# The first product in two halves of the tokens, the logarithm behind the conv's copies, and low halves put off in the last stage

## The chip, the cores and the metric

The kernel runs on one core of a Trainium2 chip. The time is device microseconds of one execution, the median over the runs shown. The core has TensorE (PE, matmuls), VectorE (DVE), ScalarE (ACT), GpSimd (POOL) and SyncE (SP, which here issues most DMAs); PEld is the load of the stationary operand into TensorE.

## The reference

One layer of a hybrid decoder, float32, 512 tokens of width 1024; all matrices are given in full.

```python
h = rms_norm(x, norm_g[0])
proj = h @ w_in                     # lru_x, lru_g, nsa_q, nsa_kv, nsa_gate, gla_*, merge_logit
y_a = rglru_mixer(...)              # conv of width 4, gates, linear recurrence, times gelu gate
y_b = nsa_mixer(...)                # compressed, selected and window attention, 16 heads
y_c = gla_mixer(...)                # gated linear attention in chunks of 32, with log_sigmoid decay
merged = sum of sigmoid(merge gate) * (y @ w_branch)
x = x + rms_norm(merged @ w_out, norm_g[1])
h = rms_norm(x, norm_g[2])
gt, up = split(h @ w_ffn_in)        # each 512 x 2816
x = x + rms_norm((silu(gt) * up) @ w_ffn_out, norm_g[3])
```

## The kernel before

Every operand of a product is split into two parts, a rounded high half (`hi`, `hh`, `whi`, made by a cast on ScalarE) and the remainder (`lo`, `hl`, `wlo`, made by a subtraction on VectorE or GpSimd), and each product is three matmuls that accumulate in one PSUM tile: high x high, high x low, low x high (`mm3`, whose three matmuls are L122, L123 and L124). Weights come as tiles of 128 x 1024 by DMA (`wraw`), from a pool of few buffers; each is cast (`whi`) and its remainder made (`wlo`) before TensorE can use it.

**The start** (L252 to L319, and L704 to L707). SP loads the four token tiles `xt` of 128 x 1024, then the two halves `ck_raw` of the first weight. For each token tile ScalarE sums the squares (`square`) and takes the root, VectorE makes the factor and scales the tile (`root`), and TensorE turns it in eight transposes into eight PSUM tiles `tps`, one for each 128 features, of 512 tokens each. Six matmuls on zeros (L304) stand behind the first tile's transposes. When all four tiles are turned, `hh` (ScalarE) and `hl` (VectorE) are evicted in eight instructions of 512 columns each, and then 48 matmuls of 512 columns make the first product, the keys of the compressed branch. The order in this block is the one written (`manual_schedule`); elsewhere a scheduler orders the instructions of each engine by priority and readiness.

**The recurrence's stage** goes over four pairs of channel tiles (`cp` 0 to 3). Streams of matmuls (`stream_t`) have other engines' work hung between their steps. For a pair, `conv` copies the projected input out of PSUM (L995, ScalarE), adds three shifted products (L1000, VectorE), casts (`xh`, L1002) and subtracts (`xl`, L1004), and TensorE makes the gates from both (`rips`). `z_exp` and `z_log` (L1068, L1072) are the two parts of the decay's log-sigmoid for the linear attention, four tiles of 512 columns each; both are hung on the last matmul stream of the round `cp` = 2. A change of the function of ScalarE between groups needs a table load.

**The last stage.** The products of the FFN's input are combined from seven smaller ones per tile pair (`winograd`, `product` at L1707 and L1710, 256 columns each; `after` gathers the results, where `fy` is the sum at L1719). When these run out, the product with `w_ffn_out` begins, in the same scheme: `tile_a` loads two blocks of the weight, `tile_b` a sum made earlier (`rows_d`) and makes a difference of `tile_a`'s two blocks (L1806), `pair` loads two blocks, and `split_u` casts the tile (L1779) and makes its low half (L1782). `weights()` hands out a tile and prepares up to three ahead; `use` runs the matmuls of a half tile into accumulators `acc`. In the program's order the low half of a tile stands directly behind its cast, except in one short stretch that a list `late` holds back. `fetch2` loads operands `r2` through SP, `second` splits them, `gb3` is the last norm's gain. At the end `store` writes eight blocks of 128 x 512, by ScalarE's queue for the first half of the columns and SP's for the second.

Of the kernel before, what the change touches and what calls it, by code (L numbers as in the profile page):

```python
# [14 lines left out]
OP = mybir.AluOpType  # L15
# [47 lines left out]
def hybrid_block_kernel(ctx, tc, x, rel_table, norm_g, w_in, conv_w, conv_b, lru_w_gates, lru_b_gates,  # L63
# [186 lines left out]
    with tc.tile_pool(name="pre", bufs=1) as pp:  # L250
        xts = [pp.tile([128, D], F32, name=f"xt{tb}") for tb in range(TB)]
        for tb in range(TB):  # L252
            sy.dma_start(xts[tb], x[0, tb * 128:(tb + 1) * 128, :])
        g8 = pp.tile([8, 128], F32, name="g8")
# [6 lines left out]
        for i in range(WARM):  # L261
# [4 lines left out]
        tps = [p.tile([128, S], F32, name="tps", tag=t) for p, t in  # L266
               ((pg, "g"), (po, "o"), (pt, "pt"), (pt, "pt"), (pa, "a"), (pa, "a"), (pa, "a"), (pa, "a"))]
        ck_raw = [load_raw([(lambda t: t.rearrange("p (k c) -> p k c", k=4),
                             dap(w_in, kh * 512 * INW + K_CMP, [[INW, 128], [128 * INW, 4], [1, 256]]))])
                  for kh in range(2)]  # L270
        ck = []

        def ck_split(kh):
            ck.append([t.rearrange("p (k c) -> p k c", k=4) for t in split_w(ck_raw[kh], v_)])

        with tc.manual_schedule(engines={mybir.EngineType.PE, mybir.EngineType.DVE, mybir.EngineType.Activation}):
            sss, ms, rs_ = [], [], []
# [9 lines left out]
            def root(tb):  # L287

                xt, m = xts[tb], ms[tb]
                r = pp.tile([128, 1], F32, name=f"r{tb}")  # L290
                t = pp.tile([128, 1], F32, name=f"t{tb}")
                a_.activation(r, m, AF.Sqrt)
                v_.reciprocal(r, r)
                v_.scalar_tensor_tensor(t, r, r[:, 0:1], m, op0=OP.mult, op1=OP.mult)
                v_.tensor_scalar(t, t, -0.5, 1.5, op0=OP.mult, op1=OP.add)
                v_.tensor_scalar(xt, xt, r[:, 0:1], t[:, 0:1], op0=OP.mult, op1=OP.mult)
                for ft in range(8):
                    pe.transpose(tps[ft][:, tb * 128:(tb + 1) * 128], xt[:, ft * 128:(ft + 1) * 128], ident)

            square(0)  # L300
            root(0)

            for i in range(WARM2):
                pe.matmul(tps[7][:, 384:512], wz, wz, start=True, stop=True)  # L304
            square(1)
            for tb in range(2, TB):
                square(tb)
                root(tb - 1)
# [3 lines left out]
            root(TB - 1)  # L312
            ck_split(0)
            for ft in range(8):
                a_.activation(hh[:, ft], tps[ft], AF.Copy, scale=g0[:, ft:ft + 1])
                v_.scalar_tensor_tensor(hl[:, ft], tps[ft], g0[:, ft:ft + 1], f(hh[:, ft]), op0=OP.mult,  # L316
                                        op1=OP.subtract)
                if ft == 3:
                    ck_split(1)  # L319
# [384 lines left out]

    ps0 = psum_t()
    for kh, n, k in [(0, n, k) for k in range(4) for n in range(2)] + [(1, n, k) for n in range(2) for k in range(4)]:
        (h, l), kk, c = ck[kh], kh * 4 + k, slice(n * 128, n * 128 + 128)  # L707
        mm3(ps0[n], h[:, k, c], l[:, k, c], hh[:, kk], hl[:, kk], kk == 0, kk == 7)
# [279 lines left out]
    def conv(cp, pss):  # L988
# [4 lines left out]
        for j, ps in enumerate(pss):  # L993
            ct = 2 * cp + j
            a_.activation(xc[:, j], ps, AF.Identity, scale=par[:, 24 + ct:25 + ct], bias=par[:, 32 + ct:33 + ct])  # L995
        for j, ps in enumerate(pss):
# [85 lines left out]
    for cp in range(4):  # L1082
# [4 lines left out]
        conv(cp, px)  # L1087
# [8 lines left out]
        if cp == 0:  # L1096
            lru_params()
        pm = stream_t(Y[:2], chain(lambda: lru_tanh(cp), *([z_products] if cp == 2 else [])),
                      chain(lambda: lru_exp(cp), *([z_exp, z_log] if cp == 2 else [])))
# [510 lines left out]
    fq = []  # L1610

    def f_cast(i):
        if i < len(floads):
# [7 lines left out]
    def f_lo(i):  # L1621
        if i < len(floads):
# [144 lines left out]
    late = []  # L1767

# [7 lines left out]
    def split_u(raw, n=1024):  # L1776
# [7 lines left out]
        if late:  # L1784
            late.append(low)
        else:
            low()
        return hi, lw

# [268 lines left out]
```

## Time and profile before

| | |
|---|---|
| median of 3 runs | 1201.88 us (1201.55 to 1203.12) |
| profiled execution | 1202.26 us, span 1200.6 us |
| mean granted clock of TensorE | 0.996 of full speed |
| busy: PE, PEld | 1180.5 us (98%), 1009.9 us (84%) |
| busy: DVE, ACT, POOL | 726.3 us (60%), 607.0 us (51%), 256.6 us (21%) |
| DMA | 219.30 MB, mean 183 GB/s |

The profile is of one execution; its times count from the span's start, and 1.7 us lie outside the span. A wait in it is the idle time of an engine before an instruction, put down to what came last. The end of a matmul is modelled: one of 512 columns shows 0.39 us busy, and the next starts before that is over, so the pace is read from starts. A matmul that begins after a wait shows a longer time, as it refills the pipeline. [...] The share of busy time covers stages that differ: at the start, in the conv and at the end TensorE waits, elsewhere hardly.

### The profile page before, as it was taken

The numbers are of one execution on the slowest core, as the hardware profiler recorded it, in microseconds if no ns is written. First come the engines' busy times: TensorE is split into PE (matmuls) and PEld (weight loads), VectorE is DVE, ScalarE is ACT, GpSimd is POOL, SyncE is SP. The second block draws the span as 40 slices with busy tenths as digits, with TensorE's granted clock in tenths as the row PEclk, the third lists the DMA queues.
The fourth block names the chain that finished last, engine by engine and source line by source line (L and its number), as shares of the span: only waits on it lengthen the run. The fifth ranks groups of instructions, "written<-read, shape, count | busy, mean of one in ns | idle before, by whom it ended". The sixth has DMA issues, their size and how long they took to land. (4 is left out here: it accounts for less than half of the span.)

```text
span 1200.6 us, 19226 instructions
## 1 busy us (share of the span) xinstructions
PE 1180.5 (98%) x7114; PEld 1009.9 (84%) x7114; DVE 726.3 (60%) x1417; ACT 607.0 (51%) x1165; POOL 256.6 (21%) x327
## 2 busy tenths in 40 slices
PE   9999999999999999999999999999999999989996
PEld 7898888888888878888888888887989999987785
DVE  6615556555467769465544353446786777765777
ACT  5326656565387677453434233234455565644553
POOL 1224555566213213222122222200000000000000
PEclk9999999999999999999999999999999999999999
DMA  8872765551469947885487989944246667667753
GB/s 259 236 217 83 195 222 196 179 163 40 115 153 228 246 151 215 202 201 150 132 203 179 212 196 236 214 149 134 85 123 189 207 202 212 197 193 239 244 184 123
DMA packets 203743, 219.30 MB, mean 183 GB/s; under 512 B 29170, under 2 KB 169694, under 8 KB 201424
## 3 DMA queue, kind: packets, MB, share of 16 engines
q1 hardware_dynamic: 189120, 170.87, 46.7%
q0 software_dynamic: 13936, 46.14, 18.3%
q8 instruction: 56, 0.92, 0.3%
q10 hardware_dynamic: 592, 1.05, 0.2%
q14 instruction: 39, 0.32, 0.1%
HBM read 209.83 MB, written 77.41 MB: 239 GB/s over the span
## 5 line engine op out<-in xcount | busy, mean ns | idle before, releaser
L92 DVE TENSOR_TENSOR wlo<-wraw,whi 128x1024 fp32r<-128x1024 f32 x91 | 111.8, 1233 | 113.6 <-ACT whi L91 86.9
L91 ACT CAST whi<-wraw 128x1024 fp32r<-128x1024 f32 x113 | 117.9, 1048 | 118.7 <-PE gps L897 29.6
L870 POOL COPY tick<-whi 128x1 f32<-128x1 f32 x76 | 53.8, 708 | 340.4 <-ACT whi L91 340.4
L894 PE MATMUL gps<-hh,whi 128*128 128x512 f32 x320 | 126.0, 394 | 0.0
L897 PE MATMUL gps<-hl,whi 128*128 128x512 f32 x320 | 124.5, 389 | 0.0
L1625 DVE TENSOR_TENSOR wlo<-wraw,whi 128x1024 fp32r<-128x1024 f32 x67 | 81.9, 1222 | 14.5 <-ACT whi L1616 14.0
L676 DVE COPY psb<-ptp 128x512 f32<-128x512 f32 (+2 forms) x72 | 45.4, 631 | 64.2 <-PE ptp L672 60.5
L637 ACT ACTIVATE p<-p,mx 128x384 f32<-128x384 f32 (+3 forms) x128 | 68.7, 539 | 26.7 <-DVE mx L635 26.5
L894 PE MATMUL gps<-hh,wlo 128*128 128x512 f32 x320 | 79.1, 389 | 0.0
L1616 ACT CAST whi<-wraw 128x1024 fp32r<-128x1024 f32 x67 | 70.3, 1049 | 13.4 <-DMA wraw<-t_d 12.0
L651 POOL TENSOR_TENSOR p<-p,sc 128x256 f32<-128x256 f32 (+3 forms) x64 | 76.5, 1217 | 1.9
L894 PE MATMUL gps<-yh,whi 128*128 128x512 f32 x192 | 74.9, 390 | 0.0
L897 PE MATMUL gps<-yl,whi 128*128 128x512 f32 x192 | 74.7, 389 | 0.0
L122 PE MATMUL gps<-hh,whi 128*128 128x512 f32 (+1 forms) x176 | 73.4, 418 | 0.8 <-DVE hl L316 0.8
L894 PEld LDWEIGHTS gps<-hh,wlo 128*128 128x128 f32 x320 | 60.1, 188 | 12.5
L894 PEld LDWEIGHTS gps<-hh,whi 128*128 128x128 f32 x320 | 60.1, 188 | 12.4
L897 PEld LDWEIGHTS gps<-hl,whi 128*128 128x128 f32 x320 | 60.1, 188 | 12.3
L122 PE MATMUL gps<-whi,hh 128*128 128x512 f32 (+1 forms) x192 | 69.9, 364 | 0.0
L124 PE MATMUL gps<-whi,hl 128*128 128x512 f32 (+1 forms) x192 | 68.1, 354 | 0.0
L123 PE MATMUL gps<-wlo,hh 128*128 128x512 f32 (+1 forms) x192 | 68.0, 354 | 0.0
L124 PE MATMUL gps<-hh,wlo 128*128 128x512 f32 (+1 forms) x176 | 65.7, 374 | 0.0
L123 PE MATMUL gps<-hl,whi 128*128 128x512 f32 (+1 forms) x176 | 65.5, 372 | 0.0
(442 smaller groups left out, 3061.8 us busy)
## 6 DMA issues: line engine op xcount, KB each, us to landing
wraw<-in_w_in_dram SPq DMA_DIRECT2D x44, 512.0 KB, 6.4
t_d<-in_w_ffn_in_dram SPq DMA_DIRECT2D x32, 704.0 KB, 8.0
wraw<-t_d SPq DMA_DIRECT2D x72, 256.0 KB, 3.2
wraw<-in_w_ffn_in_dram SPq DMA_DIRECT2D x70, 256.0 KB, 3.8
wraw<-in_w_in_dram SPq DMA_DIRECT2D x64, 256.0 KB, 4.5
t_d<-in_w_ffn_in_dram POOLq DMA_DIRECT2D x16, 704.0 KB, 9.2
rows_d<-in_w_ffn_out_dram POOLq DMA_DIRECT2D x22, 512.0 KB, 5.2
t_d<-t_d POOLq DMA_DIRECT2D x16, 704.0 KB, 8.2
```

The source lines that it names most:

```text
L91: a_.copy(hi, raw)
L92: lo_eng.tensor_tensor(lo, raw, f(hi), op=OP.subtract)
L122: pe.matmul(ps, lh, rh, start=first, stop=False)
L123: pe.matmul(ps, lh, rl, start=False, stop=False)
L124: pe.matmul(ps, ll, rh, start=False, stop=last)
L637: a_.activation(o, o, AF.Exp, scale=-1.0, bias=mx[:, br, gi:gi + 1], accum_out=sm[:, br, gi:gi + 1])
L651: g_.tensor_tensor(o, o, sc[:, br][:, :, None].to_broadcast([128, 2, n]), op=OP.mult)
L870: g_.tensor_copy(tick, f(hi[:, 0, 0:1]))
L894: pe.matmul(ps[n], part_[:, k, c], ah[:, kk], start=kk == 0 and part_ is h, stop=kk == 7 and part_ is l)
L897: pe.matmul(ps[n], h[:, k, c], al[:, kk], start=False, stop=False)
L1616: a_.copy(hi, raw)
L1625: v_.tensor_tensor(lo, raw, f(hi), op=OP.subtract)
```

## The change

It has four parts. At the start the loads go in the order first two token tiles, first weight half, other two token tiles, second weight half. The first product is made in two halves of the tokens (`first(i, kh)`: token half i, weight half kh), 96 matmuls of 256 columns; the first half stands between the transposes of the first two and the last two token tiles, `high` and `low` evict 256 columns at a time, two features' tiles share one PSUM tile, and the last token tile is scaled on ScalarE instead of VectorE. In the recurrence `z_log` moves from the end of round 2 into the conv of round 3, between its copies from PSUM and its shifted products. In the last stage each low half is collected in `late` and made by `lows()`, which runs at the end of each `use` and in `f_lo`; `tile_a` now also loads `tile_b`'s sum and makes the difference; `weights()` and the square root's table load are called later, `fetch2` elsewhere with four buffers for three. The stores go by SP but for one.

```diff
+        ck_raw = []
         for tb in range(TB):
             sy.dma_start(xts[tb], x[0, tb * 128:(tb + 1) * 128, :])
+            if tb % 2:
+                ck_raw.append(load_raw([(lambda t: t.rearrange("p (k c) -> p k c", k=4),
+                                         dap(w_in, tb // 2 * 512 * INW + K_CMP,
+                                             [[INW, 128], [128 * INW, 4], [1, 256]]))]))
         g8 = pp.tile([8, 128], F32, name="g8")
         a_.dma_start(g8, dap(norm_g, 0, [[128, 8], [1, 128]]))
...
-        tps = [p.tile([128, S], F32, name="tps", tag=t) for p, t in
-               ((pg, "g"), (po, "o"), (pt, "pt"), (pt, "pt"), (pa, "a"), (pa, "a"), (pa, "a"), (pa, "a"))]
+        tps = [[p.tile([128, 2, 256], F32, name="tps", tag=t) for p, t in banks] for banks in
+               (((pa, "a"), (pa, "a"), (pa, "a"), (pa, "a")), ((pt, "pt"), (pt, "pt"), (pa, "a"), (pa, "a")))]
...
             def root(tb):
-
-                xt, m = xts[tb], ms[tb]
                 r = pp.tile([128, 1], F32, name=f"r{tb}")
+                a_.activation(r, ms[tb], AF.Sqrt)
+                rs_.append(r)
+
+            def scale(tb):
+
+                xt, m, r = xts[tb], ms[tb], rs_[tb]
                 t = pp.tile([128, 1], F32, name=f"t{tb}")
-                a_.activation(r, m, AF.Sqrt)
                 v_.reciprocal(r, r)
                 v_.scalar_tensor_tensor(t, r, r[:, 0:1], m, op0=OP.mult, op1=OP.mult)
                 v_.tensor_scalar(t, t, -0.5, 1.5, op0=OP.mult, op1=OP.add)
-                v_.tensor_scalar(xt, xt, r[:, 0:1], t[:, 0:1], op0=OP.mult, op1=OP.mult)
+                if tb < TB - 1:
+                    v_.tensor_scalar(xt, xt, r[:, 0:1], t[:, 0:1], op0=OP.mult, op1=OP.mult)
+                else:
+                    v_.tensor_tensor(r, r, t, op=OP.mult)
+                    a_.activation(xt, xt, AF.Copy, scale=r[:, 0:1])
+
+            def turned(tb):
                 for ft in range(8):
-                    pe.transpose(tps[ft][:, tb * 128:(tb + 1) * 128], xt[:, ft * 128:(ft + 1) * 128], ident)
+                    pe.transpose(tps[tb // 2][ft // 2][:, ft % 2, tb % 2 * 128:tb % 2 * 128 + 128],
+                                 xts[tb][:, ft * 128:(ft + 1) * 128], ident)
+
+            def high(i, *fts):
+                for ft in fts:
+                    a_.activation(hh[:, ft, i * 256:i * 256 + 256], tps[i][ft // 2][:, ft % 2], AF.Copy,
+                                  scale=g0[:, ft:ft + 1])
+
+            def low(i, *fts):
+                for ft in fts:
+                    t = slice(i * 256, i * 256 + 256)
+                    v_.scalar_tensor_tensor(hl[:, ft, t], tps[i][ft // 2][:, ft % 2], g0[:, ft:ft + 1],
+                                            f(hh[:, ft, t]), op0=OP.mult, op1=OP.subtract)
+
+            def first(i, kh):
+                (h, l), t = ck[kh], slice(i * 256, i * 256 + 256)
+                for k, n in [(k, n) for k in range(4) for n in range(2)]:
+                    c, kk = slice(n * 128, n * 128 + 128), kh * 4 + k
+                    mm3(ps0[n][:, t], h[:, k, c], l[:, k, c], hh[:, kk, t], hl[:, kk, t], i + kk == 0, i == 1 and kk == 7)
 
             square(0)
             root(0)
+            scale(0)
+            turned(0)
 
             for i in range(WARM2):
-                pe.matmul(tps[7][:, 384:512], wz, wz, start=True, stop=True)
+                pe.matmul(tps[1][1][:, 1, 128:256], wz, wz, start=True, stop=True)
             square(1)
-            for tb in range(2, TB):
-                square(tb)
-                root(tb - 1)
+            root(1)
+            scale(1)
+            turned(1)
+            ck_cast(0)
+            square(2)
+            ck_low(0)
+            high(0, 0, 1)
+            low(0, 0, 1)
+            root(2)
+            high(0, 2, 3)
+            low(0, 2, 3)
+            first(0, 0)
+            square(3)
+            scale(2)
+            turned(2)
+            ck_cast(1)
+            high(0, 4, 5)
+            ck_low(1)
+            root(3)
+            low(0, 4, 5)
+            high(0, 6, 7)
+            low(0, 6, 7)
+            first(0, 1)
 
             for j8 in range(2):
                 g_.tensor_copy(M[:, 4 * j8, 0:1], xts[TB - 1][:, 0:1])
-            root(TB - 1)
-            ck_split(0)
+            scale(3)
+            turned(3)
             for ft in range(8):
-                a_.activation(hh[:, ft], tps[ft], AF.Copy, scale=g0[:, ft:ft + 1])
-                v_.scalar_tensor_tensor(hl[:, ft], tps[ft], g0[:, ft:ft + 1], f(hh[:, ft]), op0=OP.mult,
-                                        op1=OP.subtract)
-                if ft == 3:
-                    ck_split(1)
+                high(1, ft)
...
-
-    ps0 = psum_t()
-    for kh, n, k in [(0, n, k) for k in range(4) for n in range(2)] + [(1, n, k) for n in range(2) for k in range(4)]:
-        (h, l), kk, c = ck[kh], kh * 4 + k, slice(n * 128, n * 128 + 128)
-        mm3(ps0[n], h[:, k, c], l[:, k, c], hh[:, kk], hl[:, kk], kk == 0, kk == 7)
...
-    def conv(cp, pss):
+    def conv(cp, pss, then=None):
...
             a_.activation(xc[:, j], ps, AF.Identity, scale=par[:, 24 + ct:25 + ct], bias=par[:, 32 + ct:33 + ct])
+        if then:
+            then()
         for j, ps in enumerate(pss):
...
-        conv(cp, px)
+        conv(cp, px, z_log if cp == 3 else None)
...
         pm = stream_t(Y[:2], chain(lambda: lru_tanh(cp), *([z_products] if cp == 2 else [])),
-                      chain(lambda: lru_exp(cp), *([z_exp, z_log] if cp == 2 else [])))
+                      chain(lambda: lru_exp(cp), *([z_exp] if cp == 2 else [])))
...
     fq = []
+    late = []
+
+    def lows():
+        while late:
+            late.pop(0)()
 
     def f_cast(i):
+        if i >= len(floads) + 2:
+            return
         if i < len(floads):
...
             ahead(i - len(floads) + 1)
 
     def f_lo(i):
+        lows()
...
         def low():
             v_.tensor_tensor(lw[:, :n], raw[:, :n], f(hi[:, :n]), op=OP.subtract)
 
-        if late:
-            late.append(low)
-        else:
-            low()
+        late.append(low)
         return hi, lw
...
     def tile_a(k):
 
-        t = last["a"] = raw_tile()
+        t, tb_ = raw_tile(), raw_tile()
         sy.dma_start(t[:, 0:512], wsrc(k, 0))
         sy.dma_start(t[:, 512:1024], wsrc(NK + k, 1))
+        sy.dma_start(tb_[:, 0:512], rows_d[k * 128:k * 128 + 128, 512:1024])
+        v_.tensor_tensor(tb_[:, 512:1024], t[:, 0:512], t[:, 512:1024], op=OP.subtract)
+        last["b"] = tb_
         return split_u(t)
 
     def tile_b(k):
 
-        t, ab = raw_tile(), last["a"]
-        sy.dma_start(t[:, 0:512], rows_d[k * 128:k * 128 + 128, 512:1024])
-        v_.tensor_tensor(t[:, 512:1024], ab[:, 0:512], ab[:, 512:1024], op=OP.subtract)
-        return split_u(t)
+        return split_u(last["b"])
 
     def pair(src):
...
             mm3(bk[tt], ls[:, 0, sl, c], ls[:, 1, sl, c], wh, wl, k == 0, k == NK - 1)
+        lows()
...
     p2, p5 = [[p.tile([128, 512], F32, name="acc", tag=n) for _ in range(2)] for p, n in ((pa, "a"), (pt, "pt"))]
-    w = weights()
-    use(p5, LS1[0], 2, w, 1, 0)
+    lows()
+    use(p5, LS1[0], 2, done[0], 1, 0)
     y_half(2 * NK - 1, 0, "C", "u2")
     winograd(len(seq) - 2)
     after(*seq[-2])
-    use(p2, LS1[0], 1, w, 0, 0)
+    use(p2, LS1[0], 1, done[0], 0, 0)
     winograd(len(seq) - 1)
     after(*seq[-1])
-    a_.activation(cst[:, 2:3], cst[:, 0:1], AF.Sqrt)
+    weights()
...
     def fetch2(k):
         if k < NK - 1:
-            raw2[k] = fr.tile([128, 3, 256], F32, name="r2", bufs=3)
+            raw2[k] = fr.tile([128, 3, 256], F32, name="r2", bufs=4)
             sy.dma_start(raw2[k], raw2_d[:, k])
...
         v_.scalar_tensor_tensor(o, gained[tb, hf], rss[tb][1][:, 0:1], xres[tb, hf], op0=OP.mult, op1=OP.add)
-        (sy if hf else a_).dma_start(out[0, tb * 128:(tb + 1) * 128, c], o)
+        (a_ if (tb, hf) == (1, 1) else sy).dma_start(out[0, tb * 128:(tb + 1) * 128, c], o)
...
-    fetch2(0)
-    fetch2(1)
     for k in range(NK):
...
         if k == 4:
             second(NK - 1)
-        fetch2(k + 2)
+        if k == 0:
+            fetch2(0)
+        fetch2(k + 1)
+        if k == NK - 1:
+            a_.activation(cst[:, 2:3], cst[:, 0:1], AF.Sqrt)
...
             use(p7, LS2[k], 1, w, k % 2, k)
         if p == 1:
 
-            late.append(None)
...
             mean(2 + p)
         if p == 2:
-            for low in late[1:]:
-                low()
             store(2, 0)
             store(2, 1)
```

TensorE at the start of the program: `wz` are the zeros, `xt_112` to `xt_115` the four token tiles, `gps` the first product. The order before:

```order
L263 MATMUL gp_125<-ident,g_120 128x8
L298 MATMUL tps<-ident,xt_112 128x128 x8
L304 MATMUL tps<-wz 128x128 x6
L298 MATMUL tps<-ident,xt_113 128x128 x8
L298 MATMUL tps<-ident,xt_114 128x128 x8
L298 MATMUL tps<-ident,xt_115 128x128 x8
L122 MATMUL gps<-hh,whi 128x512
L123 MATMUL gps<-hl,whi 128x512
```

The order now (`hh,whi 128x512` at L164 belongs to the product after the first):

```order
L319 MATMUL tps<-ident,xt_112 128x128 x8
L345 MATMUL tps<-wz 128x128 x6
L319 MATMUL tps<-ident,xt_113 128x128 x8
L122 MATMUL gps<-hh,whi 128x256
L123 MATMUL gps<-hl,whi 128x256
L124 MATMUL gps<-hh,wlo 128x256
...
L319 MATMUL tps<-ident,xt_114 128x128 x8
L122 MATMUL gps<-hh,whi 128x256
...
L319 MATMUL tps<-ident,xt_115 128x128 x8
L122 MATMUL gps<-hh,whi 128x256
L164 MATMUL gps<-hh,whi 128x512 x2
L123 MATMUL gps<-hl,whi 128x256
```

The first product's matmuls, 256 columns wide, now stand in front of the transposes of the third and the fourth token tile, and behind the last transposes matmuls of the next product (L164) come between those of the first.

ScalarE in the recurrence's round 3: `yf` at the line with a table load directly ahead are the logarithms, `xc` the conv's copies, `xh` its cast. The order before:

```order
L1068 ACTIVATE yf<-yf 128x512 x4
L1072 ACT_TABLE_LOAD
L1072 ACTIVATE yf<-yf,cst 128x512 x4
L91 CAST whi<-wraw 128x1024
L1047 ACT_TABLE_LOAD
L1047 ACTIVATE a_4787<-a_4787 128x1024
L91 CAST whi<-wraw 128x1024
L984 CAST gwh<-gwr 128x512
L995 ACTIVATE xc<-gps,par 128x512 x2
L1002 CAST xh<-xc 128x512 x2
```

The order now:

```order
L1125 ACTIVATE yf<-yf 128x512 x4
L91 CAST whi<-wraw 128x1024
L1104 ACT_TABLE_LOAD
L1104 ACTIVATE a_4852<-a_4852 128x1024
L91 CAST whi<-wraw 128x1024
L1039 CAST gwh<-gwr 128x512
L1050 ACTIVATE xc<-gps,par 128x512 x2
L1129 ACT_TABLE_LOAD
L1129 ACTIVATE yf<-yf,cst 128x512 x4
L1059 CAST xh<-xc 128x512 x2
```

The table load and the four logarithms stood ahead of the root for the recurrence (`a`); they now stand behind the copies `xc` and ahead of the cast `xh`.

VectorE where the FFN's last input products end: `fy` are the sums that free TensorE's accumulators, `wlo<-wraw` low halves (at L1625, in the new kernel L1690, of FFN input weights, at L1782 or L1845 of W_ffn_out), `wraw<-wraw` the difference of two blocks. The order before:

```order
L1487 TENSOR_TENSOR am<-am 128x512
L1782 TENSOR_TENSOR wlo<-wraw,whi 128x1024
L1751 SCALAR_TENSOR_TENSOR am<-fy,fsg 128x512
L1806 TENSOR_TENSOR wraw<-wraw 128x512
L1782 TENSOR_TENSOR wlo<-wraw,whi 128x1024 x2
L1719 TENSOR_TENSOR fy<-wc,u_10699 128x256
L1719 TENSOR_TENSOR fy<-wa,p_10586 128x256
L1806 TENSOR_TENSOR wraw<-wraw 128x512
L1782 TENSOR_TENSOR wlo<-wraw,whi 128x1024
```

The order now:

```order
L1551 TENSOR_TENSOR lsf<-am,lsf 128x1024
L1690 TENSOR_TENSOR wlo<-wraw,whi 128x1024
L1544 TENSOR_TENSOR am<-am 128x512
L1862 TENSOR_TENSOR wraw<-wraw 128x512
L1845 TENSOR_TENSOR wlo<-wraw,whi 128x1024
L1816 SCALAR_TENSOR_TENSOR am<-fy,fsg 128x512
L1784 TENSOR_TENSOR fy<-wc,u_10767 128x256
L1784 TENSOR_TENSOR fy<-wa,p_10651 128x256
L1845 TENSOR_TENSOR wlo<-wraw,whi 128x1024
L1862 TENSOR_TENSOR wraw<-wraw 128x512
```

Two low halves stood in front of the last two `fy`; now none of W_ffn_out stands between `am` and these two, and the difference comes a place ahead of the low half in front of them.

## Rows read from the trace of the kernel before

**Rows 1.** The page's busy table: engine, busy us (share of the span), instructions.

```profile
PE 1180.5 (98%) x7114; PEld 1009.9 (84%) x7114; DVE 726.3 (60%) x1417; ACT 607.0 (51%) x1165; POOL 256.6 (21%) x327
```

**Rows 2.** TensorE's waits: us in total, times, longest us.

```profile
PE wa L1707 <- DVE fy L1719: 3.1, 1, 3.1
PE acc L123 <- DVE wlo L1782: 1.3, 3, 0.8
PE rips L123 <- DVE xl L1004: 1.3, 1, 1.3
...
PE tps L298 <- DVE xt L296: 0.7, 2, 0.3
```

**Rows 3.** Timeline of TensorE, start: start us, us busy, instruction, [idle, releaser].

```profile
13.37 1.09 PE L298 MATMUL tps<-ident,xt 128*128 128x128 f32 x8 [0.33 <-DVE xt L296]
15.27 0.50 PE L122 MATMUL gps<-hh,whi 128*128 128x512 f32 x1 [0.80 <-DVE hl L316]
```

**Rows 4.** Stretches: length, busy (instructions) by engine, granted clock, DMA share, GB/s.

```profile
15.20:26.20 11.00, 10.93 (x48) 9.08 (x49) 7.26 (x20) 6.01 (x10) 0.53 (x3) 1.00 0.64 154
...
1079.16:1082.57 3.41, 3.24 (x14) 3.15 (x15) 0.71 (x2) 0.28 (x1) 0.00 (x0) 0.50 0.23 80
1082.57:1126.00 43.43, 41.51 (x172) 31.25 (x171) 27.61 (x30) 21.44 (x25) 0.00 (x0) 1.00 0.74 246
```

**Rows 5.** Groups by line and shape, 13 to 24 us: busy us, mean ns, idle.

```profile
L316 DVE SCALAR_TENSOR_TENSOR hl<-tps,g,hh 128x512 fp32r<-128x512 f32 x8 | 5.4, 744 | 0.0
...
L315 ACT ACTIVATE hh<-tps,g 128x512 fp32r<-128x512 f32 x8 | 4.9, 704 | 2.0 <-PE tps L298 2.0
```

**Rows 6.** Groups by line and shape, 26.5 to 31.5 us.

```profile
L421 DVE COPY x<-gps 64x256 f32<-64x256 f32 x2 | 0.8, 421 | 1.7 <-PE gps L124 1.3 <-ACT x L421 0.4
L421 ACT COPY x<-gps 64x256 f32<-64x256 f32 x2 | 0.7, 366 | 1.2 <-DVE x L421 1.2
```

**Rows 7.** Timeline of ScalarE, the recurrence's round 3.

```profile
430.50 1.28 ACT L1072 ACT_TABLE_LOAD   x1
431.79 2.56 ACT L1072 ACTIVATE yf<-yf,cst 128x512 f32<-128x512 f32 x4
...
446.49 0.62 ACT L1002 CAST xh<-xc 128x512 fp32r<-128x512 f32 x1 [6.01 <-DVE xc L1000]
```

**Rows 8.** Timeline of VectorE, the same round.

```profile
435.33 1.23 DVE L92 TENSOR_TENSOR wlo<-wraw,whi 128x1024 fp32r<-128x1024 f32 x1 [4.48 <-ACT whi L91]
```

**Rows 9.** Timeline of TensorE, the end of the FFN's input products.

```profile
1073.25 0.28 PE L1707 MATMUL wa<-hh,whi 128*128 128x256 f32 x1
...
1074.68 0.40 PE L122 MATMUL acc<-whi,ls 128*128 128x512 f32 x1
...
1075.84 0.39 PE L124 MATMUL acc<-whi,ls 128*128 128x512 f32 x1
1079.33 0.58 PE L1707 MATMUL wa<-hh,whi 128*128 128x256 f32 x1 [3.10 <-DVE fy L1719]
...
1082.05 0.63 PE L122 MATMUL acc<-whi,ls 128*128 128x512 f32 x1
...
1096.66 0.51 PE L122 MATMUL acc<-whi,ls 128*128 128x512 f32 x1 [0.55 <-ACT whi L1779]
1097.92 0.51 PE L123 MATMUL acc<-wlo,ls 128*128 128x512 f32 x1 [0.76 <-DVE wlo L1782]
```

**Rows 10.** Timeline of VectorE there.

```profile
1077.38 1.23 DVE L1782 TENSOR_TENSOR wlo<-wraw,whi 128x1024 fp32r<-128x1024 f32 x1 [1.90 <-ACT whi L1779]
1078.53 0.42 DVE L1719 TENSOR_TENSOR fy<-wc,u 128x256 f32<-128x256 f32 x1
...
1079.19 0.68 DVE L1806 TENSOR_TENSOR wraw<-wraw 128x512 f32<-128x512 f32 x1
```

**Rows 11.** Timeline of ScalarE there.

```profile
1095.56 1.05 ACT L1779 CAST whi<-wraw 128x1024 fp32r<-128x1024 f32 x1 [3.60 <-DMA wraw<-in_w_ffn_out_dram]
```

**Rows 12.** Timeline of SP's queue there.

```profile
1088.86 0.54 SPq L1799 DMA_DIRECT2D wraw<-in_w_ffn_out_dram  x1
```

More of the change, by code (lines that the diff above doesn't have):

```diff
@@ L264, in hybrid_block_kernel, with ck_cast, ck_low @@
         v_.tensor_copy(g0, gp8[:, 0:8])
-        tps = [p.tile([128, S], F32, name="tps", tag=t) for p, t in
-               ((pg, "g"), (po, "o"), (pt, "pt"), (pt, "pt"), (pa, "a"), (pa, "a"), (pa, "a"), (pa, "a"))]
-        ck_raw = [load_raw([(lambda t: t.rearrange("p (k c) -> p k c", k=4),
-                             dap(w_in, kh * 512 * INW + K_CMP, [[INW, 128], [128 * INW, 4], [1, 256]]))])
-                  for kh in range(2)]
-        ck = []
-        def ck_split(kh):
-            ck.append([t.rearrange("p (k c) -> p k c", k=4) for t in split_w(ck_raw[kh], v_)])
+        tps = [[p.tile([128, 2, 256], F32, name="tps", tag=t) for p, t in banks] for banks in
+               (((pa, "a"), (pa, "a"), (pa, "a"), (pa, "a")), ((pt, "pt"), (pt, "pt"), (pa, "a"), (pa, "a")))]
+        ck = []
+        def ck_cast(kh):
+            hi = wpool.tile([128, 1024], F32R, name="whi")
+            lo = wpool.tile([128, 1024], F32R, name="wlo")
+            a_.copy(hi, ck_raw[kh])
+            ck.append((hi, lo))
+        def ck_low(kh):
+            hi, lo = ck[kh]
+            v_.tensor_tensor(lo, ck_raw[kh], f(hi), op=OP.subtract)
+            ck[kh] = [t.rearrange("p (k c) -> p k c", k=4) for t in ck[kh]]
         with tc.manual_schedule(engines={mybir.EngineType.PE, mybir.EngineType.DVE, mybir.EngineType.Activation}):
-            sss, ms, rs_ = [], [], []
+            ps0 = psum_t()
+            ms, rs_ = [], []
             def square(tb):
@@ L310, in hybrid_block_kernel @@
+            ck_low(1)
[4 more added lines that the diff above has]
+            first(0, 1)
             for j8 in range(2):
                 g_.tensor_copy(M[:, 4 * j8, 0:1], xts[TB - 1][:, 0:1])
-            root(TB - 1)
-            ck_split(0)
+            scale(3)
+            turned(3)
             for ft in range(8):
-                a_.activation(hh[:, ft], tps[ft], AF.Copy, scale=g0[:, ft:ft + 1])
-                v_.scalar_tensor_tensor(hl[:, ft], tps[ft], g0[:, ft:ft + 1], f(hh[:, ft]), op0=OP.mult,
-                                        op1=OP.subtract)
-                if ft == 3:
-                    ck_split(1)
+                high(1, ft)
+                low(1, ft)
@@ L321, in small_consts @@
+            first(1, 0)
+            first(1, 1)
     def small_consts(pp):
@@ L1766, in hybrid_block_kernel @@
     raws = [0]
-    late = []
     def raw_tile():
```

## Prediction

> **What bounds the kernel now.** I read the busy table first: TensorE is busy for 1180.5 us, 98% of the span [rows 1]. A change can therefore win in two ways only, by taking a wait from TensorE or by letting it run at its higher clock where it does not, and it can lose by adding matmul time. So the next view is the list of TensorE's waits [rows 2]: the longest is one of 3.1 us for a VectorE result `fy` near the end of the program, then three for a low half `wlo` (1.3 together), one for the conv's low half `xl` (1.3), and two for the normalised input `xt` (0.7). The waits on semaphores before the first product add 0.80 [rows 3]. Each of these lies in a place that the change touches, so the sum is made place by place from the timelines there. [...]
>
> **The start: the first product in halves.** Before, TensorE turns the four token tiles, waits 0.33, 0.33 and 0.80 on the way (the two of 0.33 are the 0.7 of [rows 2], the last is in [rows 3]), and from 15.27 us runs 48 matmuls in 10.93 us, 0.228 each [rows 4]. The waits sum to 1.46. After it, 96 matmuls of 256 columns. The nearest row for one is the winograd group near the end: 12 matmuls from 1073.25 to 1074.68, 0.119 each [rows 9]. So 96 x 0.119 = 11.4 us, 0.5 more than before.
> What can be won is the 1.46 us. I walked the new order by durations. The transposes of tile 1 take about as long as now (8 in 1.09 [rows 3]); then the first matmul needs one eviction `hh` of 256 columns, the second an `hl`. No row shows these; the nearest are a copy of 256 columns at 0.366 on ScalarE and 0.421 on VectorE [rows 6], and the same evictions at 512 columns, 0.704 and 0.744 [rows 5]. I take 0.48 for either, nearer to the copy plus what scaling adds. The first matmul so waits some 0.5 for `hh`, the next 0.5 for `hl`; the transposes of tile 2 wait some 0.2 for `xt`, the second four feature tiles 0.5 for `hl` behind the second `wlo` on VectorE, and those of tile 3 some 0.3 for the scaling that now runs on ScalarE. That is 2.0 us in place of 1.46: the waits are cut into more and smaller pieces, not removed. In the second half eight pairs `hh`, `hl` feed the matmuls, 0.48 + 0.48 for 0.71 us of matmuls (6 x 0.119) when they follow each other on one PSUM tile; the order puts matmuls of the next product between them, which covers it. The small loads that come later on SP can hold the conv of the compressed keys by some tenths. Sum: 0.5 + 0.5, less a little for cover: **+0.9 us**. Bounds: all waits gone, 0.5 - 1.46 = -1.0; and without the cover 8 x 0.25 = 2.0 on top, +2.9.
> A row speaks for a price of halving: 256 columns cost VectorE 0.421 and 512 cost 0.744, so two halves are 0.1 dearer than a whole [rows 5, 6]. [...]
>
> **The logarithm `z_log` moved behind the conv's copies.** Before, ScalarE runs a table load (1.28) and four logarithms (2.56) at 430.50 [rows 7], and everything behind them waits: VectorE idles 4.48 us before the `wlo` at 435.33 [rows 8], then the scan of the recurrence, the gate product and the conv follow on it, and the cast `xh` comes only after ScalarE idled 6.01 us [rows 7]. TensorE waits 1.30 for `xl` at the end of this chain [rows 2]. Taken out there, the chain comes 3.8 us earlier (1.28 + 2.56); the same 3.8 us now lie on ScalarE inside its idle 6.01, before `xh`. The next limit is the end of the stream of matmuls that TensorE is busy with until then, so only the wait goes: **-1.3 us**, bounds 0 (`xh` is late behind the logarithms) and -1.3.
>
> **The end: low halves put off.** Before, two low halves stand on VectorE ahead of the two `fy` sums. The second starts at 1077.38 after an idle 1.90 us for its cast on ScalarE; `fy` follows at 1078.53 [rows 10], and TensorE, whose last matmul before was at 1075.84, starts again at 1079.33 [rows 9]. The wait depends on the queue's order, not on VectorE's load. After it, `fy` stands ahead of that low half, and its own inputs have been ready since TensorE's last product. So the wait of 3.1 goes. Late next is the low half of the first tile of W_ffn_out: ahead of it VectorE has a `wlo` (1.23) and a difference (0.68), both in [rows 10], and then it takes 1.23 itself. I estimate 0.8 us of wait there, where 0.2 is today: +0.6.
> Without the long idle I expect the clock to stay at 1.00. Price by rows: the 12 matmuls of 256 columns from 1079.33 to 1082.05 took 2.72 us where the 12 before took 1.43 [rows 9], 1.3; with the first wide ones behind it 1.5. So -1.5. The trace's rows are that the clock fell during the wait of 3.1 and did not through the one of 0.80 at the start. [...]
> From 1082.57 to 1126.00, 172 matmuls take 43.43 us [rows 4]; at 0.228 they would take 39.2. Of the 4.2 over, 0.55 + 0.76 at 1096.66 and 1097.92 [rows 9], with 0.1 of refilling for each, belong to a tile whose load landed late: ScalarE waited 3.60 for it [rows 11], and it was issued at 1088.86 [rows 12] behind the norm's gain and three loads of `r`. The order keeps these four ahead of it, so 1.5 stays. The other 2.6 are small waits on `wlo` and casts; since the difference is now made a tile earlier and the low half is queued later, I count two thirds as gone: -1.7, bounds 0 and -2.6. Moving the square root's table load out of this stretch takes 1.28 from ScalarE in front of a cast; that is inside the same sum.
> End together: -3.1 + 0.6 - 1.5 - 1.7 = **-5.7 us**; bounds -1.5 (the long wait halves, the clock still falls) and -7.0.
>
> **The tail.** Stores go almost all by SP; issuing a transfer takes SP about half a microsecond [rows 12], no more than VectorE needs for a block of the result. ScalarE is freed of issues that nothing waits for. **0**, bounds 0.3 either way.
>
> **Sum.** The profiled execution took 1202.26 us, 1.7 more than its span and 0.4 more than the median of the runs. 1202.26 + 0.9 - 1.3 - 5.7 = 1196.2; less 0.4, **1195.8 us**.
>
> **The rivals.** *First, the forecast*: about 1195.8, own range 1193 to 1198.5. *Second, the loads rule the end*: `fy` comes early, but TensorE then waits as long for a tile of W_ffn_out, because these tiles are read on SP behind the same big transfers; the clock falls again. For it: the load in [rows 11]. Against it: that load is needed some 17 us after the long wait. Then 1202.26 + 0.9 - 1.3 - 0.4 = 1201.5. *Third, the start is dear and the small waits stay*: +2.9 at the start and -4.0 at the end: 1202.26 + 2.9 - 1.3 - 4.0 - 0.4 = 1199.5. For it: the fixed price of halves [rows 5, 6]; against it: the cover in the order. *Fourth, the clock falls in the start*: the first 48 small matmuls run between waits, at 0.227 (2.72 / 12) for 0.119, 5.2 us more: 1201.0. Against it: 0.80 us of idle did not do it before, and no wait I expect is longer. *Fifth, slower: the low halves come late*. The stage has eleven pairs of tiles of W_ffn_out and of rows made from it; a low half that now stands behind the next tile's difference (0.68) would come that much later, with 0.1 of refilling, at each pair: 11 x 0.79 = 8.7, so 1195.8 + 8.7 = 1204.5. It decides from the point at which TensorE reaches the second matmul of a tile before the low half is done. Against it: VectorE idles for the cast before such a half [rows 10], so it has room.
>
> **Chances.** Forecast 0.70, third 0.12, second 0.08, fourth 0.05, fifth 0.05. What a measurement can tell from no change is 0.2%, 2.4 us, so faster means under 1199.5. The third case lies on that line and is halved; I shift a little from the forecast, as its end term rests on an estimate of a wait that no row shows: faster 0.78, same 0.16, slower 0.06. Range 1191.5 to 1201: its lower end is the forecast with the better bounds of end and start together in part, its upper end reaches the second and fourth cases.
>
> **What would show it.** At the start: the first matmul of 256 columns near 12 us instead of 15.27, waits on `hl` and `hh` between, and the end of the first product no earlier than now. At the conv: no wait of TensorE for `xl`, and the logarithms inside ScalarE's gap before `xh`. At the end: no wait for `fy`, the granted clock 1.00 throughout, a wait under 1 us for the first `wlo` of the stage, and the late load still there some 20 us on. It is wrong if TensorE's waits in the first 35 us fall below 1 us, or if a wait of over 2 us stands anywhere behind the last product of the FFN's input.

## The result, and the profile after

Six runs of each kernel: 1195.53 us (1195.26 to 1197.66) against 1202.02 (1201.09 to 1203.12), ratio 0.9948 with a 95% interval of 0.9936 to 0.9961. The forecast was 1195.8 us. The profiled execution took 1195.47 us, span 1193.8.

The sum came out, its terms less well. Reading when the same matmul starts in both traces, counted back from the last one, gives the account by place:

| place | forecast | measured in the traces |
|---|---|---|
| start, up to the compressed keys' products | +0.9 | +2.0 |
| conv of round 3 | -1.3 | -1.6 |
| last stage | -5.7 | -7.0 |
| behind the last matmul | 0 | -0.2 |

The expectations below were written with +2.2 for the start; the two traces give +1.98. The start also moves from run to run: in the fourteen traces of this document, one and the same matmul behind it lies up to 0.7 us apart among those with the old start and up to 0.6 among those with the new one as the change has it. So its cost is known to a few tenths only.

TensorE's waits of the changed kernel, in the columns of [rows 2]:

```profile
PE acc L123 <- DVE wlo L1845: 1.7, 3, 0.8
PE tps L319 <- ACT xt L315: 1.5, 1, 1.5
PE gp L267 <- DVE wz L262: 1.2, 1, 1.2
PE gps L123 <- DVE hl L330: 0.8, 2, 0.5
PE acc L122 <- ACT whi L1842: 0.4, 1, 0.4
```

The waits for `fy` and for `xl` are gone. New is one of 1.5 us for the last token tile, in the start. The timeline of TensorE there, against [rows 3]:

```profile
11.27 0.38 PE L122 MATMUL gps<-hh,whi 128*128 128x256 f32 x1
12.16 0.39 PE L123 MATMUL gps<-hl,whi 128*128 128x256 f32 x1 [0.50 <-DVE hl L330]
...
16.57 0.39 PE L123 MATMUL gps<-hl,whi 128*128 128x256 f32 x1 [0.32 <-DVE hl L330]
...
21.07 1.09 PE L319 MATMUL tps<-ident,xt 128*128 128x128 f32 x8 [1.48 <-ACT xt L315]
```

The first product starts at 11.27 instead of 15.27, but waits of 0.50, 0.32 and 1.48 follow, 2.3 in place of 1.46. That is 0.8 of the 2.0; 0.5 are the 96 matmuls, and the other 0.7 are refilling, which is the name here for the longer time of a matmul behind a wait (0.39 us at 12.16 and 16.57 where those that follow show 0.28), and small gaps, which I did not take apart. VectorE shows where the long one is from; then GpSimd in the same stretch:

```profile
17.61 0.16 DVE L308 RECIPROCAL r<-r 128x1 f32<-128x1 f32 x1
17.80 1.57 DVE L309 SCALAR_TENSOR_TENSOR t<-r,m 128x1 f32<-128x1 f32 x1
19.40 0.15 DVE L310 TENSOR_SCALAR t<-t 128x1 f32<-128x1 f32 x1
```

```profile
16.95 2.40 POOL L92 TENSOR_TENSOR wlo<-wraw,whi 128x1024 fp32r<-128x1024 f32 x1 [6.64 <-ACT whi L91]
```

An instruction of one column took 1.57 us where its sister for the tile before took 0.22. It ended at 19.37, GpSimd's subtraction at 19.35. In the kernel before, that subtraction ran from 25.86 us on, behind all of this chain.

In the conv ScalarE does the logarithms where it idled before [rows 7]:

```profile
439.68 1.28 ACT L1129 ACT_TABLE_LOAD   x1
440.97 2.56 ACT L1129 ACTIVATE yf<-yf,cst 128x512 f32<-128x512 f32 x4
444.83 0.62 ACT L1059 CAST xh<-xc 128x512 fp32r<-128x512 f32 x1 [1.29 <-DVE xc L1057]
```

Its idle time before `xh` is 1.29 instead of 6.01, and `xh` stands 1.66 earlier although the whole stage began 2.0 later. At the end, TensorE's timeline against [rows 9], then VectorE's against [rows 10], then the stretches against [rows 4]:

```profile
1071.89 0.39 PE L122 MATMUL acc<-whi,ls 128*128 128x512 f32 x1
1072.97 0.50 PE L123 MATMUL acc<-wlo,ls 128*128 128x512 f32 x1 [0.70 <-DVE wlo L1845]
...
1076.83 0.39 PE L124 MATMUL acc<-whi,ls 128*128 128x512 f32 x1
1077.05 0.28 PE L1772 MATMUL wa<-hh,whi 128*128 128x256 f32 x1
...
1092.71 0.50 PE L122 MATMUL acc<-whi,ls 128*128 128x512 f32 x1 [0.42 <-ACT whi L1842]
1093.97 0.50 PE L123 MATMUL acc<-wlo,ls 128*128 128x512 f32 x1 [0.76 <-DVE wlo L1845]
```

```profile
1071.10 0.68 DVE L1862 TENSOR_TENSOR wraw<-wraw 128x512 f32<-128x512 f32 x1
1071.70 1.22 DVE L1845 TENSOR_TENSOR wlo<-wraw,whi 128x1024 fp32r<-128x1024 f32 x1
...
1075.87 0.42 DVE L1784 TENSOR_TENSOR fy<-wa,p 128x256 f32<-128x256 f32 x1 [2.01 <-PE wa L1772]
```

```profile
1074.00:1091.80 17.80, 17.80 (x91) 15.15 (x90) 9.28 (x12) 5.52 (x7) 0.00 (x0) 1.00 0.74 242
1091.80:1095.30 3.50, 2.32 (x10) 1.34 (x9) 3.14 (x4) 3.39 (x4) 0.00 (x0) 1.00 0.74 276
1095.30:1120.00 24.70, 24.70 (x109) 20.22 (x108) 20.59 (x23) 13.62 (x17) 0.00 (x0) 1.00 0.92 302
```

VectorE now waits for TensorE before `fy` (2.01) and not the reverse; the products run on at 1077.05; the clock stays at 1.00; the wait at the first `wlo` is there (0.70, and 0.50 us for that matmul where others show 0.39), and so is the late tile at 1092 us. Between 1095.3 and 1120 TensorE is busy throughout: all the small waits went, of which I had counted two thirds.

### The profile page after: what moved, and what is told of

It reads as the page before. It is cut to its first block, busy times and chain, and to the rows that moved or that the text cites. A ratio compares the mean times of both kernels' runs of the same rounds, so it can differ in the third digit from the quotient of the medians.

```text
span 1193.8 us, 19335 instructions
## 1 busy us (share of the span) xinstructions
PE 1177.6 (99%) x7162; PEld 1012.1 (85%) x7162; DVE 728.4 (61%) x1425; ACT 610.0 (51%) x1174; POOL 256.2 (21%) x327
## 4 chain that ended last, share of the span: by engine, by line
PE 94%; DVE 3%; ACT 1%; issue 1%; DMA 1%; SPq 0%; DVEq 0%; ACTq 0%
PE gps L949 19%; PE gps L952 10%; PE gps L122 8%; PE gps L123 7%; PE gps L124 7%; PE wa L1772 6%; PE ops L754 4%; PE s L686 3%; PE wa L1775 3%; PE ptp L732 3%; PE wc L1772 3%; PE acc L123 2%; PE acc L124 2%; PE acc L122 2%; PE gps L164 2%; PE wb L1772 1%
## 5 line engine op out<-in xcount | busy, mean ns | idle before, releaser
L92 DVE TENSOR_TENSOR wlo<-wraw,whi 128x1024 fp32r<-128x1024 f32 x89 | 109.4, 1233 | 113.7 <-ACT whi L91 84.3
L1690 DVE TENSOR_TENSOR wlo<-wraw,whi 128x1024 fp32r<-128x1024 f32 x67 | 81.9, 1223 | 14.0 <-ACT whi L1680 13.4
L122 PE MATMUL gps<-hh,whi 128*128 128x512 f32 (+1 forms) x192 | 76.6, 399 | 0.0
L123 PE MATMUL gps<-hl,whi 128*128 128x512 f32 (+1 forms) x192 | 68.7, 358 | 0.8 <-DVE hl L330 0.8
L124 PE MATMUL gps<-hh,wlo 128*128 128x512 f32 (+1 forms) x192 | 68.6, 357 | 0.0
```

The costliest lines, as they stand in the source:

```text
L92: lo_eng.tensor_tensor(lo, raw, f(hi), op=OP.subtract)
L122: pe.matmul(ps, lh, rh, start=first, stop=False)
L123: pe.matmul(ps, lh, rl, start=False, stop=False)
L124: pe.matmul(ps, ll, rh, start=False, stop=last)
L1690: v_.tensor_tensor(lo, raw, f(hi), op=OP.subtract)
```

## The experiments

Each ran in five rounds beside the kernel before; times are medians, ratios are to the kernel before. What had to be told apart: what the start costs and why, and which of the last stage's edits moved `fy`.

**The old start in the changed kernel.** All edits of the start are undone.

> The changed kernel with the start of the kernel before (four token tiles first, then 48 matmuls of 512 columns); the rest as changed. Theory: the new start costs 2.2 us, since from the end of the first product on every matmul of the changed kernel stands 2.19 us later than before, and nothing behind it depends on how the start is made. Then 1195.5 - 2.2 = 1193.3 us, and the parts in conv and last stage keep their -1.6 and -7.0. Rival: the later stages gain because the loads of the start come in another order; then the old start gives back some of it and the time lies at 1195 or above.

1196.52 us (1194.51 to 1197.68), ratio 0.9949 (0.9936 to 0.9962): by the time alone the expectation failed. The trace shows why. The stretches at the late tile:

```profile
1080.00:1092.39 12.39, 10.74 (x47) 8.35 (x46) 6.92 (x9) 4.73 (x6) 0.00 (x0) 0.99 0.90 318
1092.39:1095.81 3.42, 3.42 (x10) 2.66 (x9) 3.42 (x5) 1.05 (x1) 0.00 (x0) 0.53 0.69 208
```

```profile
1090.66 0.49 PE L122 MATMUL acc<-whi,ls 128*128 128x512 f32 x1 [0.88 <-ACT whi L1787]
1091.92 0.56 PE L123 MATMUL acc<-wlo,ls 128*128 128x512 f32 x1 [0.77 <-DVE wlo L1790]
```

Here the wait for the late tile is longer (0.88 and 0.77 where the changed kernel shows 0.42 and 0.76), and the clock falls behind it, to 0.53 over 3.42 us. The first tile's `acc` stands 2.5 us earlier than in the changed kernel, near the 2.2 expected; the late tile takes 2.0 of it back. So this wait, which I had let stand at 1.5 us, costs 2.1 here and 3.3 in the longest case below, from start to start and without what the clock adds, and it blurs each comparison by median.

**The new start alone**, in the kernel before.

> The kernel before with the new start alone. Theory: +2.2 us on 1202.0, so 1204.2: 0.5 for 96 matmuls at 0.119 instead of 48 at 0.228, the waits of 0.65, 0.45 and 1.5 for the 1.95 of before (counted from start to start), and some tenths in the small fp32 products behind. Rival: the start costs nothing by itself and the 2.2 come from the other parts: 1202.

1204.60 us, ratio 1.0018 (1.0009 to 1.0027), +2.3: the start by itself makes the kernel slower, by about what the account says; behind the start the matmuls of this trace stand 2.1 later than before. Again one instruction of one column takes 1.39 us and ends at 19.50, GpSimd's subtraction at 19.49.

**One tensor input.** For the last token tile:

```diff
-                v_.scalar_tensor_tensor(t, r, r[:, 0:1], m, op0=OP.mult, op1=OP.mult)
+                if tb < TB - 1:
+                    v_.scalar_tensor_tensor(t, r, r[:, 0:1], m, op0=OP.mult, op1=OP.mult)
+                else:
+                    v_.tensor_scalar(t, r, r[:, 0:1], m[:, 0:1], op0=OP.mult, op1=OP.mult)
...
-                    v_.tensor_tensor(r, r, t, op=OP.mult)
+                    v_.tensor_scalar(r, r, t[:, 0:1], None, op0=OP.mult)
```

> The changed kernel; for the last token tile two VectorE instructions of one column are written with a pointer scalar instead of a second tensor in SBUF (t = r*r*m and r = r*t), same arithmetic. In the changed kernel the first of them took 1.57 us where its three sisters took 0.22, and it ended when a subtraction on GpSimd (16.95 to 19.35) ended. Theory: VectorE's second tensor input waits for GpSimd's whole instruction; with one tensor input the chain runs through, the wait of 1.5 us before the last transposes falls to 0.1 to 0.3, and the time is 1.2 to 1.4 us lower: 1194.2. Rival a: any VectorE instruction with both operands in SBUF or a scalar pointer is held just the same: 1195.5, the instruction still shows 1.5 us. Rival b: the chain was late for another reason and the next instruction takes the wait over: 1195.5 with the wait elsewhere.

1193.87 us, ratio 0.9934 (0.9921 to 0.9948). VectorE, then GpSimd in this run:

```profile
17.55 0.15 DVE L308 RECIPROCAL r<-r 128x1 f32<-128x1 f32 x1
17.73 0.27 DVE L312 TENSOR_SCALAR t<-r,m 128x1 f32<-128x1 f32 x1
18.04 0.15 DVE L313 TENSOR_SCALAR t<-t 128x1 f32<-128x1 f32 x1
18.23 0.21 DVE L317 TENSOR_SCALAR r<-r,t 128x1 f32<-128x1 f32 x1
```

```profile
16.89 2.40 POOL L92 TENSOR_TENSOR wlo<-wraw,whi 128x1024 fp32r<-128x1024 f32 x1 [5.26 <-ACT whi L91]
```

All four ran inside GpSimd's 2.40 us; TensorE's wait for `xt` fell from 1.5 to 0.2, and behind the start the matmuls stand 1.3 earlier than in the changed kernel. Nothing else was edited, so it was the form with a second tensor input that was held up.

**The logarithm alone**, in the kernel before.

> The kernel before with the logarithm moved alone. Theory: the wait of TensorE for the conv's low half (1.46 us from start to start and 0.11 refill) goes and nothing else moves: 1202.0 - 1.6 = 1200.4. Rival: the recurrence's stage has slack elsewhere and the gain needs the other parts: 1202.

1200.61 us, ratio 0.9987 (0.9978 to 0.9996), -1.7. The part stands by itself.

**The first tile handed out early again**, in the changed kernel:

```diff
-    lows()
-    use(p5, LS1[0], 2, done[0], 1, 0)
+    w = weights()
+    lows()
+    use(p5, LS1[0], 2, w, 1, 0)
...
-    use(p2, LS1[0], 1, done[0], 0, 0)
+    use(p2, LS1[0], 1, w, 0, 0)
...
-    weights()
```

> The changed kernel with one edit of the last stage undone: the first tile of W_ffn_out is handed out (and so the tiles three ahead prepared) before the last two products of the FFN's input, as in the kernel before; the deferred low halves and the earlier difference stay. Theory a: this call alone sets where the low halves stand against the sums fy, since the scheduler orders VectorE by priority and readiness; the wait of 3.1 us for fy and the half clock come back: +4.8, 1200.3, granted clock 0.50 for some 3.4 us. Theory b (my prediction): the deferral removes the wait; then it stays away and the time is 1195.5 within 0.5.

1198.92 us, ratio 0.9975 (0.9965 to 0.9986). The wait is back, with the deferral in place:

```profile
PE wa L1772 <- DVE fy L1784: 3.1, 1, 3.1
```

The granted clock is 0.50 for 3.41 us from 1080.12; its mean over this execution is 0.995, against 0.998 in the changed kernel's. It costs 3.4 instead of 4.8, and the late tile's wait is only 0.5 here from start to start, where the changed kernel has 1.6.

**The differences made late again**, `tile_a` and `tile_b` as before.

> The changed kernel with the tile of differences loaded and made where it is split, as before. Theory a: the earlier difference is what removed the seven small waits on low halves between 1100 and 1126 us (2.6 with their refills) and it cost the 0.86 at the first tile for 0.26: 2.6 - 0.6 = +2.0, 1197.5. Theory b: the deferral removed the small waits: 1195.0, since only the 0.6 comes back.

1198.76 us, ratio 0.9969 (0.9960 to 0.9979). The wait at the first tile is 0.26 again as expected, and waits of 1.8 with their refills are back at 1117 and 1122 us; the rest of the +3.2 is the late tile (a wait of 1.1 for its cast and 0.8 for its low half) with the clock's fall behind it (mean 0.997 over the execution, 0.998 in the changed kernel's). Theory a by direction; its size is mixed with the other effect. In the kernel before, half of the small waits (1.2 of 2.5) lie behind 1115 us and half ahead of it. Those behind it stand in every trace with the late differences and in none with the early ones. Those ahead of it are not back in this run; they are missing as well in the other two traces with late differences in which the clock fell at the late tile (the start alone, the hand-out alone). What removed that half is therefore not separated.

**No deferral**: each low half behind its cast in the program.

```diff
-        late.append(low)
+        low()
```

> The changed kernel with each low half made directly behind its cast in the program (the list is never filled); all else as changed. Theory a: the scheduler gives nearly the same order on VectorE, so 1195.5 within 0.3. Theory b (my prediction's step): the deferral is what brings fy ahead; without it the wait of 3.1 us, the half clock and small waits come back: 1200 to 1202.

1195.89 us (1195.02 to 1197.76), ratio 0.9952 (0.9940 to 0.9965), and no wait for `fy`. TensorE's waits in the profiled execution, the slowest of the five:

```profile
PE acc L122 <- ACT whi L1842: 1.7, 1, 1.7
PE acc L123 <- DVE wlo L1845: 1.5, 2, 0.8
```

The first is the late tile, and the clock falls behind it (mean 0.996 over the execution, 0.998 in the changed kernel's). The small waits behind 1115 us do not come back. The edit that I named as the cause is worth nothing that shows in the time.

**The hand-out alone**, in the kernel before.

> The kernel before with one edit of the last stage: the first tile is taken from the ready list and the next hand-out moved behind the last two products of the FFN's input. Theory: this edit alone removes the wait for fy (3.26 from start to start) and the half clock behind it (1.5); the tiles are then prepared later, so the late tile's wait grows and may take the clock down, and the small waits stay: -2.5 to -4.8, 1197.3 to 1199.5. Rival (my prediction's step): without the deferral the wait for fy stays: 1202.

1199.65 us, ratio 0.9979 (0.9970 to 0.9988). The waits in its trace that belong to the last stage:

```profile
PE acc L122 <- ACT whi L1779: 2.1, 1, 2.1
PE acc L123 <- DVE wlo L1782: 1.8, 3, 0.8
```

No wait for `fy`: this one edit takes it away. Much of the gain goes to the late tile, now 2.1 and 0.8, with the clock at 0.50 behind it from 1094.9 (mean 0.995 over the execution).

**Gain and operands later**, on the kernel with the old start:

```diff
-    sy.dma_start(gb3, dap(norm_g, 3 * D, [[0, 128], [1, D]]))
...
-        if k == 0:
-            fetch2(0)
-        fetch2(k + 1)
+        fetch2(k)
+        if k == 3:
+            sy.dma_start(gb3, dap(norm_g, 3 * D, [[0, 128], [1, D]]))
```

> The kernel of e1_old_start with the last norm's gain loaded three tiles later and the operands r one at a time, one iteration later each; nothing else. Theory: the tile of W_ffn_out that TensorE waits for at 1092 us (0.58 + 1.03 + 0.11 from start to start) is late because 512 KB of gain and three loads of r stand ahead of it on SP; with two r ahead it lands in time: 1.3 to 1.7 less than e1, 1191.7. Rival: the tile is late because its buffer comes free late or the DMA engines are full with other transfers; then as e1, 1193.3.

1191.63 us (1191.42 to 1191.86), ratio 0.9915 (0.9901 to 0.9928). SP's queue in the run with the old start, where the tile's second block (L1805) stands behind the gain `gb` and three loads of `r`, and then in this run:

```profile
1080.56 0.33 SPq L1878 DMA_DIRECT2D gb<-in_norm_g_dram  x1
1080.94 1.79 SPq L1885 DMA_DIRECT2D r<-raw_d  x3
1082.77 0.66 SPq L1805 DMA_DIRECT2D wraw<-in_w_ffn_out_dram  x1
```

```profile
1080.62 0.33 SPq L1804 DMA_DIRECT2D wraw<-in_w_ffn_out_dram  x1
1081.27 2.03 SPq L1884 DMA_DIRECT2D r<-raw_d  x2
1083.34 0.43 SPq L1805 DMA_DIRECT2D wraw<-in_w_ffn_out_dram  x1
```

ScalarE's cast of the tile, in the same two runs:

```profile
1089.56 1.99 ACT L1787 CAST whi<-wraw 128x1024 fp32r<-128x1024 f32 x2 [4.40 <-DMA wraw<-in_w_ffn_out_dram]
```

```profile
1087.84 2.00 ACT L1787 CAST whi<-wraw 128x1024 fp32r<-128x1024 f32 x2 [1.78 <-PE acc L124]
```

No wait of TensorE for that tile is left, the clock is 1.00 to the last matmul (mean 0.998 over the execution, 0.996 in the run with the old start), and the runs lie within 0.4 us where most versions with the wait spread over 2 to 3. The block is not issued earlier, 1083.34 against 1082.77; it lands sooner, since the cast waits 4.40 us for it in the one run and not for a load at all in the other. So the moment of its issue does not explain it; what differs is the transfers in front of it. Whether the gain or the third `r` matters more was not separated.

**The same with the new start**, and then with one tensor input as well.

> The changed kernel, new start kept, with the last norm's gain and the operands r loaded later as in e8_gain_later. Theory: the wait for the late tile (1.7 with refill in the changed kernel's profile, up to 2.9 in others) goes whatever the start is, and with it the half clock that follows it in some executions: 1195.5 - 1.7 = 1193.8, with a narrow spread. The difference to e8 is then the start alone, 2.2. Rival: what e8 gained came from the old start and the moved loads together; then 1195.

> e9_gain_later_new_start with the two one-column instructions of e3_one_input. Theory: e9 less the 1.2 to 1.4 that e3 showed: 1192.5, so the new start without the blocked instruction costs some 0.9 against e8 (the value I predicted for the start). Rival: the new start is as good as the old one once it is not blocked: 1191.6.

1193.26 us, ratio 0.9924 (0.9911 to 0.9938), and 1192.32 us, ratio 0.9916 (0.9902 to 0.9929). Without the late tile the start can be read from medians: it costs 1.6 against the old one, and 0.7 once VectorE's one-column instruction is not held up (0.27 us in the run above with one tensor input, in place of 1.57). The old start was measured in an earlier group of runs, but the traces agree: right behind the start the difference is 1.7 and 0.6.

**The first low half ahead of the difference**, on the kernel of the moved loads with the old start:

```diff
+        u = split_u(t)
+        if k == 0:
+            lows()
         v_.tensor_tensor(tb_[:, 512:1024], t[:, 0:512], t[:, 512:1024], op=OP.subtract)
         last["b"] = tb_
-        return split_u(t)
+        return u
```

> e8_gain_later; for the first tile of W_ffn_out alone the low half is made before the difference of its blocks. Theory: the 0.86 us wait before the second matmul of that tile falls to 0.26, as the difference (0.68) no longer stands ahead on VectorE: 1191.6 - 0.6 = 1191.0. Rival: the wait is for the cast or for the low half ahead of it, and stays: 1191.6.

1190.96 us (1190.73 to 1191.07), ratio 0.9904 (0.9891 to 0.9918): the fastest version here, 1.0% under the kernel before. The wait at the first tile is 0.26 from start to start, as before the change.

## Why the prediction was right or wrong, point by point

**The time** was right, and in part by luck, for two errors cancelled: the start cost 1.1 us more than said, the last stage gave 1.3 more.

**The start**: the mechanism was right (cut waits, dearer matmuls), the size was not. The most mis-sized term is "those of tile 3 some 0.3 for the scaling": 1.5 in the traces. With one tensor input it is 0.2, so my figure was that of a start without GpSimd. GpSimd's subtraction moves ahead in the changed kernel; I had read the orders of TensorE, ScalarE and VectorE, and did not ask what VectorE would do beside GpSimd. The traces show what it did: the same step took 1.57 and 1.39 us with two tensor inputs and 0.27 with one, each time beside a GpSimd subtraction of 2.40 us. By what means the one form is held up and the other not, no run shows. Two terms held: `hl` and `hh` at 256 columns took 0.48 each, as I said, and the 96 matmuls 0.119 each. By these rows two halves are 0.21 to 0.25 dearer than one instruction of 512 columns, not 0.1. The other waits were smaller than forecast: none for the first `hh` (0.5) and for tile 2's `xt` (0.2), 0.32 for the second `hl` (0.5). Against that stand the 0.7 of refilling and small gaps, which the forecast put at nothing here, though it counted 0.1 of refilling for each wait in the last stage.

**The logarithm**: right; the refill of 0.1 (in the kernel before, the matmul behind the wait for `xl` shows 0.50 us, others 0.39) and the start-to-start count make 1.6 of 1.3.

**The last stage, low halves put off**: the result of this step was right and its cause was wrong. I wrote that the deferral puts `fy` ahead. Undoing the deferral changes nothing, undoing the later hand-out brings the wait of 3.1 and the half clock back, and the hand-out alone removes it from the kernel before. The scheduler sets VectorE's order, and what moved `fy` is that the next tiles are asked for behind the last two products. Of the small waits, those behind 1115 us went with the earlier differences; for the others the cause is open. The stage's -7.0 is also the good bound of the prediction, but by chance: with its own terms and all small waits gone the sum is -3.1 + 0.6 - 1.5 - 2.6 = -6.6. The order that I read showed where the rows went, not which line sent them there.

**The clock**: right for this profile, 1.00 from 7.4 us to behind the last matmul. The 1.5 us belong to the wait, since they come back with it. What I missed is that the clock can fall behind the late tile as well: I counted 1.5 us for it and took it as fixed. It was 1.6 with refills in the changed kernel's profile and up to 3.3 in the others, and the clock fell behind it in the profiles of five of the eight experiments that had the wait (0.53 over 3.42 us with the old start; means of 0.995 to 0.997 over the five executions, 0.998 in the changed kernel's). Whether the changed kernel's one run of 1197.66 is such a case was not profiled.

**The tail**: from the start of the last matmul to the span's end it is 10.0 to 10.3 us in the traces with the old form of the stores and 10.0 to 10.6 with the new one, so the 0.2 is not shown to be theirs.

**The rivals**: the start went some way to its dear end (third case, +2.9), the end reached its good one, so neither alone decided. The loads (second case) did not rule the changed kernel's end, but where the late tile brings the clock down, as in the trace without deferral, they take part of the gain. The fourth case did not come: the clock stays at 1.00 through the start, with waits of 0.50, 0.32 and 1.48 between the small matmuls. The slower case did not come: no tile's low half waited behind a difference, except the first one.

## What to carry to other kernels

Where a scheduler sets the order, undo one line at a time before naming the line that moved an instruction; a list that defers work may move nothing. When a change brings a GpSimd instruction forward, look at which short VectorE instructions with two tensor inputs will stand beside it: one took 1.57 us for 0.22 here. And count a wait near the end as a risk to the clock, not only as its own length: it fell behind the late tile in five of eight experiments here, and taking two of four loads away from in front of one tile was worth 2 to 3 us with the new start and 4 to 5 with the old one, as much as the new start cost or more.

## What the runs showed of the hardware

A one-column VectorE instruction with two tensor inputs took seven times its length here, 1.57 us for 0.22, until a GpSimd subtraction ended, while a reciprocal and forms with one tensor input passed beside such a subtraction in 0.15 to 0.27. The clock's fall behind waits is not regular here: it came after waits of 0.88 and 0.77 us close together in one run (the old start, 0.53 over 3.42 us), and stayed away after 1.3 and 0.8 in another (one tensor input, mean 0.998 over the execution).
